# A norm applied behind the products, a fixed start of the program, and the sums of the last pass moved behind the last split

## The chip, the cores and the metric

One core of a Trainium2 chip runs the whole layer; nothing is exchanged with other cores. The metric is the device time of one execution in microseconds (us). The engines are TensorE (PE; its weight loads are shown apart as PEld), VectorE (DVE), ScalarE (ACT), GpSimd (POOL) and SyncE (SP), whose queue issues most of the loads.

## The reference, cut to what matters

A decoder layer over 256 positions with 2048 channels, in float32: a norm, one wide projection that feeds a recurrent branch and an attention branch, their merging, a second norm and an MLP with a norm behind it.

```python
def rmsnorm(x, g):
    y = xf * lax.rsqrt(jnp.mean(xf * xf, axis=-1, keepdims=True) + RMS_EPS)
    return y * g

h = rmsnorm(x, norm_mix_pre[l])
proj = h @ w_in[l]
xr, yr, q, k, v, g_rnn, g_attn = jnp.split(proj, IN_OFFSETS, axis=-1)
xr = rg_lru(causal_depthwise_conv(xr, conv_w, conv_b), ...)
y_rnn = xr * jax.nn.gelu(yr)
q, k = rope(q, positions), rope(k, positions)
y_att = sliding_window_sink_attention(q, k, v, sinks)
mix = sigmoid(g_rnn) * (y_rnn @ w_rnn_proj) + sigmoid(g_attn) * (y_att @ w_attn_proj)
x = x + rmsnorm(mix @ w_out, norm_mix_post)
h = rmsnorm(x, norm_mlp_pre)
u = jnp.square(jax.nn.relu(h @ w_mlp_up))
x = x + rmsnorm(u @ w_mlp_down, norm_mlp_post)
```

The first norm is a factor per position, r = 1/sqrt(mean of x squared + eps), and a gain per channel. The product `h @ w` may therefore be formed as r times the product of (x times gain) with w.

## The kernel before, in words

**Numbers as two parts.** Each float32 weight and activation is split into a high part (rounded to a shorter form that PE takes at full rate, `fp32r`) and a low part (the rest). A product is then three: high by high, high by low, low by high. Weights come as *halves* of 128x1024 from SP's queue (tile `wraw`); ACT casts each into its high part (`whi`, line 92) and DVE subtracts (`wlo`, line 93). `Stream` runs this ahead of the products by up to six halves (`AHEAD`, and six buffers each for high and low parts); a new half can be split when a product has freed a buffer.

**Order.** A scheduler puts the instructions of each engine in an order; `pin` keeps a marked instruction in the written order with other marked ones, and `tc.issue_after(x)` keeps what is inside behind x. Every engine works through its list in order, so an instruction that waits holds up all behind it.

**The head.** The two blocks of 128 positions of x (x0 and x1, 128x2048 each) are loaded, each in two halves, with the first weights between and behind them. Seven products of ones (`warm`, line 342) keep PE at work. The gain of the first norm is one row, loaded on ACT's queue (line 311), that four fp32 products with ones (`gain_b`, line 348) spread over the 128 partitions. For each block ACT and DVE sum the squares of its four quarters (lines 354 and 358), `rms` (lines 334 to 336) makes r out of them, DVE multiplies a quarter by r and the gain in one instruction (line 363), PE transposes it in four 128x128 pieces into a PSUM bank (`ptr`, line 369), ACT casts the high part of the transposed quarter out of it (line 375) and DVE subtracts the low part (line 376). The result, `hT`, feeds all projections. The first of these gives keys and values (bank `kv0` for block 0, `kv1` for block 1; lines 388, 390 and 391), and it is woven by hand into the head. The low parts of the first four weight halves are made by POOL.

**The middle.** Then come, for four groups, the gate `ga` (a product with positions on partitions; its sigmoid is a tanh of half the value) and the queries `q`; behind them the projections x and y (`px`, `py`; eight pairs each, in `conv` and `gelu`, with channels on partitions), the gates of the recurrence, the projections of both branches, `g2`-gates and the merging, the out-projection, the second norm, and the MLP. The keys are rotated by the tables `cc` and `ss` (cosine and sine, made on DVE and ACT from the positions, lines 491 to 510), transposed (`pk`, line 540) and kept for all groups. They are made by a generator, `keys_values`, that the gate's loop steps on.

**The last pass.** The MLP's down-product runs in four passes; `down(f, n, ...)` with f = 1, n = 1 is the last. Seven of its 16 chunk pairs go by Strassen-like sums into the banks P1, P6, Q5 and N7 (named `s` in the profile). When the last of these is in, DVE adds them up into four tiles `ready` (lines 1029 to 1032), `early` adds the first half's sum `acc` to each (line 1094) and loads the last gain `g3`. The last three chunk pairs are held, and are then put into the banks of the four outputs one output after the other (`dQ`, `dCs`, `dP`, `dQ`; line 987). `finish` adds a bank to its `ready` tile (line 1108), sums its squares on ACT (line 1112), multiplies by the gain (lines 1113 and 1118) and, when a block of positions is whole, makes r and writes four outputs (line 1124).

## Time and profile before

| | us |
|---|---|
| median of three runs | 1553.24 (1552.12 to 1554.74) |
| the profiled execution | 1548.21 |
| its span, from the first to the last instruction | 1546.4 |
| PE busy within the span | 1516.1 (98%) |
| DVE busy | 1098.4 (71%) |
| ACT busy | 824.0 (53%) |
| POOL busy | 12.1 (1%) |
| moved from memory | 288.60 MB, 191 GB/s over the span |

The profiled execution is one of its own, apart from the three timed runs; durations below are its durations. A busy share is a mean over all stages. What bounds a stage is read in the timelines, where the bracket behind an instruction gives the time that its engine stood idle before it and what ended that. PE's records can overlap: a product's duration is longer than the step to the next one. In the counts of instructions an fp32 product, or a product of ones, shows as two records.

### The profile page before, as it was taken

The page shows a single profiled execution, that of the slowest core. Times are in us where ns is not written, and L with a number is a line of the kernel's source. Part 1 is how long each engine was busy: PE and PEld are TensorE (multiplying, and loading weights), DVE is VectorE, ACT ScalarE, POOL GpSimd, SP SyncE. Part 2 cuts the span into 40 slices and gives each one's busy share as a digit, 9 for nine tenths or more (in the row PEclk, how much of TensorE's full clock was granted, in tenths as well). Part 3 has the DMA queues.
Part 4 walks back from the last instruction along what each step waited for, and adds up shares of the span by engine and source line. Part 5 has one row for each costly group of instructions (what it writes and reads, how often), then busy time and mean ns, then how long its engine had stood idle before and what let it go on. Part 6 is the DMA issues. An engine that isn't in the chain of part 4 may idle for free.

```text
span 1546.4 us, 19944 instructions
## 1 busy us (share of the span) xinstructions
PE 1516.1 (98%) x7562; PEld 1264.5 (82%) x7562; DVE 1098.4 (71%) x1338; ACT 824.0 (53%) x1116; POOL 12.1 (1%) x14
## 2 busy tenths in 40 slices
PE   7999999999999999999999999999999999999996
PEld 5887777788888888888877888888888888888885
DVE  5666666856759867546666876688886766678897
ACT  4545555646647757444354655555454555555552
POOL 3000000000000000000000000000000000000000
PEclk9999999999999999999999999999999999999999
DMA  6454354354655575665663865556667655576663
GB/s 247 161 179 146 127 174 155 125 185 156 227 193 175 166 222 177 203 196 184 243 237 108 271 202 185 190 182 210 215 205 234 204 188 190 181 282 193 202 212 129
DMA packets 82322, 296.19 MB, mean 192 GB/s; under 512 B 9521, under 2 KB 9777, under 8 KB 81201
## 3 DMA queue, kind: packets, MB, share of 16 engines
q1 hardware_dynamic: 78768, 285.48, 56.6%
q10 hardware_dynamic: 3458, 9.45, 1.6%
q8 instruction: 59, 0.97, 0.2%
q14 instruction: 37, 0.30, 0.1%
HBM read 288.60 MB, written 6.29 MB: 191 GB/s over the span
## 4 chain that ended last, share of the span: by engine, by line
PE 81%; DVE 8%; DMA 5%; ACT 3%; issue 2%; DVEq 0%; POOL 0%; ACTq 0%; SPq 0%; POOLq 0%
PE ps L235 21%; PE ps L238 10%; PE dQ L987 5%; DMA wraw<-in_w_dn 4%; DVE wlo L93 4%; PE dP L987 2%; PE s L987 2%; PE gr L253 2%; PE pa L253 2%; PE pr L257 2%; PE pr L255 2%; PE gr L255 2%; PE q L253 2%; PE pr L253 2%; PE gr L257 2%
## 5 line engine op out<-in xcount | busy, mean ns | idle before, releaser
L93 DVE TENSOR_TENSOR wlo<-wraw,whi 128x1024 fp32r<-128x1024 f32 x524 | 635.3, 1222 | 317.5 <-ACT whi L92 316.4
L92 ACT CAST whi<-wraw 128x1024 fp32r<-128x1024 f32 x528 | 549.3, 1050 | 582.5 <-PE ps L235 140.2
L235 PE MATMUL ps<-h2T,whi 128*128 128x512 f32 x1024 | 256.6, 392 | 0.6 <-DVE h2T L286 0.6
L235 PEld LDWEIGHTS ps<-h2T,whi 128*128 128x128 f32 x1024 | 184.2, 189 | 33.8 <-DVE h2T L286 0.8
L238 PEld LDWEIGHTS ps<-h2T,wlo 128*128 128x128 f32 x1024 | 139.7, 190 | 10.0
L238 PE MATMUL ps<-h2T,wlo 128*128 128x256 f32 x1024 | 142.8, 282 | 0.0
L235 PE MATMUL ps<-hT,whi 128*128 128x512 f32 x512 | 130.2, 394 | 0.0
L987 PE MATMUL dQ<-whi,uT 128*128 128x512 f32 x288 | 106.9, 390 | 0.0
L235 PEld LDWEIGHTS ps<-hT,whi 128*128 128x128 f32 x512 | 91.7, 189 | 18.0 <-issue 1.8
L238 PEld LDWEIGHTS ps<-hT,wlo 128*128 128x128 f32 x512 | 70.0, 190 | 5.0
L238 PE MATMUL ps<-hT,wlo 128*128 128x256 f32 x512 | 71.9, 283 | 0.0
L987 PEld LDWEIGHTS dQ<-whi,uT 128*128 128x128 f32 x288 | 54.2, 188 | 11.3 <-ACT whi L92 0.3
L987 PE MATMUL dQ<-wlo,uT 128*128 128x512 f32 x144 | 56.5, 393 | 4.6 <-DVE wlo L93 4.6
L987 PE MATMUL dCs<-whi,uT 128*128 128x512 f32 x144 | 54.5, 395 | 0.0
L112 DVE TENSOR_TENSOR tlo<-t,thi 128x1536 fp32r<-128x1536 f32 x28 | 49.2, 1756 | 7.3 <-ACT thi L111 7.1
L987 PE MATMUL dP<-whi,uT 128*128 128x512 f32 x144 | 53.8, 389 | 0.0
L253 PE MATMUL ga<-whi,hT 128*128 128x512 f32 x128 | 51.2, 400 | 0.0
L253 PE MATMUL q<-whi,hT 128*128 128x512 f32 x128 | 51.1, 399 | 0.0
L257 PE MATMUL ga<-whi,hT 128*128 128x512 f32 x128 | 50.3, 393 | 0.0
L255 PE MATMUL ga<-wlo,hT 128*128 128x512 f32 x128 | 50.3, 393 | 0.0
L255 PE MATMUL q<-wlo,hT 128*128 128x512 f32 x128 | 50.2, 392 | 0.0
L253 PE MATMUL gr<-whi,hT 128*128 128x512 f32 x128 | 50.0, 391 | 0.0
(272 smaller groups left out, 2581.3 us busy)
## 6 DMA issues: line engine op xcount, KB each, us to landing
wraw<-in_w_up SPq DMA_DIRECT2D x128, 512.0 KB, 4.6
wraw<-in_w_dn SPq DMA_DIRECT2D x128, 512.0 KB, 4.6
wraw<-in_w_g SPq DMA_DIRECT2D x64, 512.0 KB, 4.7
wraw<-in_w_xy SPq DMA_DIRECT2D x64, 512.0 KB, 4.5
wraw<-in_w_q SPq DMA_DIRECT2D x32, 512.0 KB, 4.2
wraw<-in_w_ap SPq DMA_DIRECT2D x32, 512.0 KB, 3.8
wraw<-in_w_rp SPq DMA_DIRECT2D x32, 512.0 KB, 4.4
wraw<-in_w_out SPq DMA_DIRECT2D x32, 512.0 KB, 5.0
```

The lines of the kernel that those rows point to most:

```text
L92: self.pin(self.nc.scalar.copy(hi, src))
L93: self.pin(self.low.tensor_tensor(lo, src, hi.bitcast(F32), ALU.subtract))
L112: v.tensor_tensor(lo, t, hi.bitcast(F32), ALU.subtract)
L235: mm(both, hi[:, k * P : k * P + P], a.rearrange("p a b -> p (a b)"), start=half == 0 and k == 0, stop=False)
L238: mm(ps[:, f, 1, :], lo[:, k * P : k * P + P], a[:, 0, :], start=False, stop=half == 1 and k == 7)
L253: mm(banks[tb][n], a[:, 0, t], hi[:, n * 512 : n * 512 + 512], start=first, stop=False)
L255: mm(banks[tb][n], a[:, 0, t], lo[:, n * 512 : n * 512 + 512], start=False, stop=False)
L257: mm(banks[tb][n], a[:, 1, t], hi[:, n * 512 : n * 512 + 512], start=False, stop=last)
L987: mm(b, a[x], w[y], start=not begun and i == 0, stop=tail and i == 2)
```

## The change

1. *The gain of the first norm* is now a column per tile of 128 channels (`gcol`, 128x16, a new input) and is loaded first on ACT's queue. x is transposed as it is loaded. `quad` (four instructions of 128x128, one block of positions) and `both` (two of 128x256, both blocks) take it out of the PSUM bank and multiply by the gain in the same instruction, high parts on ACT and low parts on DVE. The spreading of the gain is gone, and the scaling of x.
2. *The factor r* is applied behind the products: to the tables `cc` and `ss` (keys and queries), to the values as they are copied, as the scale of the gates' tanh (`rhalf`), and to px and py by a multiplication with `r_all`, which holds r along the free axis for every partition and is made by `spread_r`. The squares are summed behind the kv products, and only one of them in the head.
3. *The order of the head* is pinned throughout: loads, dummies (four more behind the first transposes), the kv products, and four banks by name (`front_bank`) for some of the transposes. All low parts of weights are made by DVE.
4. *In the last pass* all halves are split when the last of the seven is in, and the sums with `acc` and the multiplications with the gain are put behind the last low part.

```diff
-        self.pin(self.low.tensor_tensor(lo, src, hi.bitcast(F32), ALU.subtract))
+        self.last_low = self.pin(self.nc.vector.tensor_tensor(lo, src, hi.bitcast(F32), ALU.subtract))
...
+WARM_ON = 4
...
-    gain = flat(unit("gain", F32))
-    for q in range(4):
-        (nc.gpsimd if q == 3 else nc.vector).memset(gain[:, quarter(q)], 0.0)
-    nc.scalar.dma_start(gain[0:1, :], gains[0:1])
...
+    gcol = const.tile([P, KT], F32, name="gcol")
+    pin(nc.scalar.dma_start(gcol, g_cols))
+
+    def load_x(tb, half):
+        c = slice(half * 1024, half * 1024 + 1024)
+        return pin(nc.sync.dma_start(x_nat[tb][:, c], x_v[tb][:, c]))
+
+    ws.pin_load = pin
+    load_x(0, 0)
+    ws.load_to(1)
+    load_x(1, 0)
+    ws.load_to(4)
+    load_x(0, 1)
+    last = load_x(1, 1)
+    ws.load_to(2 * EXTRA + WRAW)
+    ws.pin_load = lambda i: i
...
-    warm = bank(psb, "warm")
-    for i in range(WARM):
-        mm(warm[:, 0:P], ones, ones, start=True, stop=True)
-    gain_b = []
-    for q in range(4):
-        if q % 2 == 0:
-            room = pair("gain_b")
-        gain_b.append(room[:, q % 2].rearrange("p a b -> p (a b)"))
-        mm(gain_b[q], ones, gain[:, quarter(q)], start=True, stop=True)
+    warm = bank(psm, "warm")
+
+    def dummies(n):
+        for i in range(n):
+            pin(mm(warm[:, 0:P], ones, ones, start=True, stop=True))
...
+    wide_banks = [pair("front") for i in range(2)]
+
+    def front_bank(i):
+        return wide_banks[i % 2][:, i // 2].rearrange("p a b -> p (a b)")
...
-    def scale(tb, q, r):
-        c = quarter(q)
-        pin(nc.vector.scalar_tensor_tensor(x_nat[tb][:, c], x_nat[tb][:, c], r, gain_b[q], ALU.mult, ALU.mult))
...
+    def turn(key, ps, tiles):
+        xT[key] = ps
+        for i, (tb, k) in enumerate(tiles):
+            pin(nc.tensor.transpose(ps[:, i * P : i * P + P], x_nat[tb][:, k * P : k * P + P], ident))
+
+    def act(k, part, t=slice(0, S)):
+        return hT[k // 4][:, k % 4, part, t]
+
+    def quad(tb, q, low):
+
+        t = slice(tb * P, tb * P + P)
         for i in range(4):
             k = 4 * q + i
-            pin(nc.tensor.transpose(ps[:, i * P : i * P + P], x_nat[tb][:, k * P : k * P + P], ident))
-
-    def part(tb, q):
-        t = slice(tb * P, tb * P + P)
-        p3 = ps_t.pop((tb, q)).rearrange("p (a b) -> p a b", a=4)
-        hi = hT[q][:, :, 0, t]
-        pin(nc.scalar.copy(hi, p3))
-        pin(nc.vector.tensor_tensor(hT[q][:, :, 1, t], p3, hi.bitcast(F32), ALU.subtract))
+            src = xT[tb, q][:, i * P : i * P + P]
+            if low:
+                pin(nc.vector.scalar_tensor_tensor(act(k, 1, t), src, gcol[:, k : k + 1], act(k, 0, t).bitcast(F32),
+                                                   ALU.mult, ALU.subtract))
+            else:
+                pin(nc.scalar.activation(act(k, 0, t), src, AF.Copy, scale=gcol[:, k : k + 1]))
+
+    def both(j, low):
+
+        for i in range(2):
+            k = 2 * j + i
+            src = xT[j][:, i * S : i * S + S]
+            if low:
+                pin(nc.vector.scalar_tensor_tensor(act(k, 1), src, gcol[:, k : k + 1], act(k, 0).bitcast(F32),
+                                                   ALU.mult, ALU.subtract))
+            else:
+                pin(nc.scalar.activation(act(k, 0), src, AF.Copy, scale=gcol[:, k : k + 1]))
 
...
+    def kv_hi(j, tb, parts=(0, 1)):
+
+        t = slice(tb * P, tb * P + P)
+        for part in parts:
+            for i in range(2):
+                kt = 2 * j + i
+                pin(mm(kv[tb][0], act(kt, part, t), held[j][0][:, quarter(i)], start=kt == 0 and part == 0,
+                       stop=False))
+
+    def kv_lo(j, tb):
+        t = slice(tb * P, tb * P + P)
+        for i in range(2):
+            kt = 2 * j + i
+            pin(mm(kv[tb][0], act(kt, 0, t), held[j][1][:, quarter(i)], start=False, stop=kt == KT - 1))
+
...
-    square(0, 0)
-    square_v(0, 1)
-    square(0, 2)
-    square_v(0, 3)
-    r = rms(0, 0)
-    ws.low = nc.gpsimd
-    scale(0, 0, r)
-    turn(0, 0)
-    scale(0, 1, r)
-    turn(0, 1)
-    scale(0, 2, r)
-    part(0, 0)
...
+    dummies(WARM)
+    for q in range(2):
+        turn((0, q), bank(psm, "front"), [(0, 4 * q + i) for i in range(4)])
+    dummies(WARM_ON)
+    quad(0, 0, False)
     split(1)
+    quad(0, 0, True)
+    square(0, 0, True)
+    kv_hi(0, 0)
+    for q in range(2):
+        turn((1, q), front_bank(q), [(1, 4 * q + i) for i in range(4)])
+    kv_lo(0, 0)
+    quad(1, 0, False)
+    quad(1, 0, True)
+    kv_hi(0, 1)
     split(2)
+    kv_hi(1, 0)
+    kv_lo(0, 1)
+    kv_lo(1, 0)
+    kv_hi(1, 1)
+    kv_lo(1, 1)
+    for tb in range(TB):
+        quad(tb, 1, False)
     split(3)
+    for tb in range(TB):
+        quad(tb, 1, True)
+    for tb in range(TB):
+        kv_hi(2, tb)
     split(4)
+    for tb in range(TB):
+        kv_lo(2, tb)
+    for j in (4, 5):
+        turn(j, front_bank(j - 2), [(tb, 2 * j + i) for i in range(2) for tb in range(TB)])
+    for tb in range(TB):
+        kv_hi(3, tb)
+    for tb in range(TB):
+        kv_lo(3, tb)
+    for j in (6, 7):
+        turn(j, bank(psm, "front"), [(tb, 2 * j + i) for i in range(2) for tb in range(TB)])
     for j in range(4, 8):
+        both(j, False)
+        split(j + 1)
+        both(j, True)
+        for tb in range(TB):
+            kv_hi(j, tb)
+        for tb in range(TB):
+            kv_lo(j, tb)
...
+    ws.pin = lambda i: i
+    ws.ahead(7)
+    for tb in range(TB):
+        for q in range(4):
+            if tb or q:
+                square(tb, q, q % 2 == 1)
+    r0 = [rms(tb, 0) for tb in range(TB)]
...
+    for tb in range(TB):
+        for t in (cc, ss):
+            nc.vector.tensor_scalar(t[:, tb], t[:, tb], r0[tb], None, ALU.mult)
+    rhalf = small("rhalf", [P, TB])
+    for tb in range(TB):
+        nc.vector.tensor_scalar(rhalf[:, tb : tb + 1], r0[tb], 0.5, None, ALU.mult)
+    r_all = small("r_all", [P, S])
+
+    def spread_r():
+        pr = bank(psm, "pr")
+        for tb in range(TB):
+            dg = t2("dg")[:, 0:P]
+            nc.vector.tensor_scalar(dg, ident, r0[tb], None, ALU.mult)
+            mm(pr[:, tb * P : tb * P + P], ones, dg, start=True, stop=True)
+        nc.scalar.copy(r_all, pr[:, 0:S])
...
-            nc.scalar.copy(v_sb[:, tb, :], banks[tb][:, 256:512])
+            nc.scalar.activation(v_sb[:, tb, :], banks[tb][:, 256:512], AF.Copy, scale=r0[tb])
...
+        spread_r()
...
-            nc.scalar.activation(m1[g][:, tb, :], gate[tb], AF.Tanh, scale=0.5)
+            nc.scalar.activation(m1[g][:, tb, :], gate[tb], AF.Tanh, scale=rhalf[:, tb : tb + 1])
...
         p3 = wide(t2("px"))
         a_pair(hT, p3)
+        nc.vector.tensor_tensor(p3, p3, r_all.unsqueeze(1).to_broadcast([P, 2, S]), ALU.mult)
...
         a_pair(hT, wide(py))
+        nc.vector.tensor_tensor(wide(py), wide(py), r_all.unsqueeze(1).to_broadcast([P, 2, S]), ALU.mult)
...
-            nc.scalar.activation(out[tb], banks[tb], AF.Tanh, scale=0.5)
+            nc.scalar.activation(out[tb], banks[tb], AF.Tanh, scale=rhalf[:, tb : tb + 1])
...
                 if p == SEVEN[-1]:
+                    if f == 1 and n == 1:
+                        ws.split_to(2 * len(chunks))
...
         def early(ready):
-            for (tb, i), t in ready.items():
-                c = quarter(2 * n + i)
-                nc.vector.tensor_tensor(t, t, acc[tb][:, c], ALU.add)
+            with tc.issue_after(ws.last_low.ins) if n == 1 else ExitStack():
+                for (tb, i), t in ready.items():
+                    c = quarter(2 * n + i)
+                    behind = nc.vector.tensor_tensor(t, t, acc[tb][:, c], ALU.add)
+                    if n == 1:
+                        ws.last_low = behind
...
             last[tb, i] = t
             if i == 0:
-                for k in range(2):
-                    c = quarter(k)
-                    nc.vector.tensor_tensor(acc[tb][:, c], acc[tb][:, c], g3[0][:, c], ALU.mult)
+                with tc.issue_after(ws.last_low.ins):
+                    for k in range(2):
+                        c = quarter(k)
+                        nc.vector.tensor_tensor(acc[tb][:, c], acc[tb][:, c], g3[0][:, c], ALU.mult)
...
+        "g_cols": np.ascontiguousarray(per_channel(g("norm_mix_pre"))),
```

In the rows below a name is out<-in with the tile's number where several stand side by side; `x3` counts equal rows, and the bracket has the engines or load queues whose signals the instruction waits for.

The head on PE, before: the gain row's products stand ahead of the first transposes (`ptr`).

```order
L342 MATMUL warm<-ones 128x128 x6
L348 MATMUL gain_b<-gain,ones 128x512 [waits DMAHW2_49,DVE_49]
L348 MATMUL gain_b<-gain,ones 128x512 [waits DVE_49] x2
L348 MATMUL gain_b<-gain,ones 128x512 [waits Pool_49]
L369 MATMUL ptr<-ident,x_76 128x128 [waits DMAHW0_49,DVE_49,Pool_49]
L369 MATMUL ptr<-ident,x_76 128x128 x3
L369 MATMUL ptr<-ident,x_76 128x128 [waits DVE_49]
L369 MATMUL ptr<-ident,x_76 128x128 x3
L390 MATMUL kv_141<-whi_169,hT_137 128x512 [waits Activation_49]
```

The same place now (`front` are the transposes' banks; x_76 is x0, x_77 is x1):

```order
L348 MATMUL warm<-ones 128x128 x6
L369 MATMUL front<-ident,x_76 128x128 [waits DMAHW1_49,Pool_49]
L369 MATMUL front<-ident,x_76 128x128 x3
L369 MATMUL front<-ident,x_76 128x128 [waits DVE_49]
L369 MATMUL front<-ident,x_76 128x128 x3
L348 MATMUL warm<-ones 128x128 x4
L411 MATMUL kv_126<-whi_153,hT_120 128x512 [waits Activation_49]
L411 MATMUL kv_126<-whi_153,hT_120 128x512 x3
L369 MATMUL front<-ident,x_77 128x128 [waits DMAHW3_49]
L369 MATMUL front<-ident,x_77 128x128 x7
```

The first transposes wait for a load and POOL's identity alone. The second four still wait for DVE: of the two banks of their pool one is held by the dummies until the last of them, so they take the bank of the first four, when its four low parts have been taken out.

The keys' place on DVE, now (wlo are low parts of weight halves; L361 are squares, L338 and L340 the norm, L525 `rhalf`, L500 and L503 the beginning of the tables):

```order
L93 TENSOR_TENSOR wlo_370<-wraw_107,whi_369 128x1024 [waits DMAHW1_49,PE_49,Activation_49]
L361 SCALAR_TENSOR_TENSOR j,sqs<-x_76 128x512 x2
L361 SCALAR_TENSOR_TENSOR j,sqs<-x_77 128x512 x2
L338 TENSOR_REDUCE st<-sqs 128x1 [waits DVE_49,Activation_49]
L93 TENSOR_TENSOR wlo_454<-wraw_109,whi_453 128x1024 [waits DMAHW2_49,PE_49]
L340 RECIPROCAL st<-st 128x1 [waits Activation_49]
L338 TENSOR_REDUCE st<-sqs 128x1
L93 TENSOR_TENSOR wlo_482<-wraw_373,whi_481 128x1024 [waits DMAHW7_49,PE_49]
L340 RECIPROCAL st<-st 128x1 [waits Activation_49]
L500 CAST posf<-pos_i 128x2 [waits DMAHW3_49]
L525 TENSOR_SCALAR rhalf<-st 128x1
```

Before, the low part ahead of the tables (L491 there) was followed by them at once. The transposes of the keys (`pk`) stand 67 products behind the first product of `ga`; before they stood 40 behind it.

The last low part on DVE, before (L1029 to L1032 are the sums, L1094 the addition of `acc`, L1118 a multiplication by the gain):

```order
L93 TENSOR_TENSOR wlo_12544<-wraw_12469,whi_12543 128x1024 [waits DMAHW0_49,Activation_49]
L1029 TENSOR_TENSOR t<-s_12047,t 128x512 [waits Activation_49]
L1118 TENSOR_TENSOR acc_11400<-acc_11400,g_12539 128x512 [waits DMAHW2_49]
L1030 TENSOR_TENSOR t<-s_12048,t 128x512 [waits DVE_49,PE_49]
L1094 TENSOR_TENSOR t<-t,acc_11401 128x512
L1031 TENSOR_TENSOR t<-t,s_12048 128x512 [waits DVE_49]
L1032 TENSOR_TENSOR t<-t,s_12048 128x512
L1094 TENSOR_TENSOR t<-t,acc_11400 128x512 [waits DVE_49]
L1094 TENSOR_TENSOR t<-t,acc_11401 128x512 [waits DVE_49]
L1094 TENSOR_TENSOR t<-t,acc_11400 128x512
L93 TENSOR_TENSOR wlo_12548<-wraw_12471,whi_12547 128x1024 [waits DMAHW1_49,Activation_49]
```

And now (L1058 to L1061 are the sums, L1124 the addition of `acc`):

```order
L93 TENSOR_TENSOR wlo_12574<-wraw_12516,whi_12573 128x1024 [waits DMAHW0_49,Activation_49]
L93 TENSOR_TENSOR wlo_12578<-wraw_12518,whi_12577 128x1024 [waits DMAHW1_49,Activation_49]
L1058 TENSOR_TENSOR t<-s_12094,t 128x512 [waits PE_49,Activation_49]
L1059 TENSOR_TENSOR t<-s_12095,t 128x512 [waits DVE_49,PE_49]
L1124 TENSOR_TENSOR t<-t,acc_11448 128x512
L1060 TENSOR_TENSOR t<-t,s_12095 128x512 [waits DVE_49]
L1061 TENSOR_TENSOR t<-t,s_12095 128x512
L1124 TENSOR_TENSOR t<-t,acc_11447 128x512 [waits DVE_49]
```

The last low part follows the one before it at once, and the sums stand behind both.

93 lines of the change are left out of this document (13 added, 80 removed).

## The prediction

> **What bounds the kernel now.** I read the busy time by stage first. The columns of this view are: stretch, its length, then busy time (and count) of PE, PEld, DVE, ACT, POOL, then the granted clock, the DMA share and GB/s.
>
> ```profile
> 0.00:48.24 48.24, 38.17 (x151) 28.75 (x151) 29.61 (x46) 22.29 (x35) 12.07 (x14) 0.93 0.59 219
> 48.24:1517.60 1469.36, 1462.35 (x7354) 1223.72 (x7352) 1048.84 (x1260) 797.59 (x1072) 0.00 (x0) 1.00 0.59 192
> 1517.60:1546.40 28.80, 15.62 (x59) 12.01 (x59) 19.99 (x34) 4.12 (x11) 0.00 (x0) 0.87 0.28 98
> ```
>
> In the middle PE is busy 1462 of 1469 us at a full clock: nothing is to be had there, only to be lost. The head (until the first gate product) and the tail (after the last sums begin) hold 10 and 13 us in which PE does nothing. So I read those two in the timelines (start, duration, instruction, idle time before it and what ended it), the head from the chain of waits on.
>
> ```profile
> 2.75 5.66 DMA gain<-in_gains
> 8.54 5.98 PE L348 MATMUL gain_b<-gain,ones 128*128 128x512 f32 x8 [4.10 <-DMA gain<-in_gains]
> 14.36 1.04 PE L369 MATMUL ptr<-ident,x 128*128 128x128 f32 x8
> 21.83 0.73 PE L388 MATMUL kv<-wlo,hT 128*128 128x512 f32 x2 [1.70 <-POOL wlo L93]
> 24.56 1.12 PE L369 MATMUL ptr<-ident,x 128*128 128x128 f32 x4 [2.00 <-DVE hT L376]
> 25.90 0.63 PE L391 MATMUL kv<-whi,hT 128*128 128x512 f32 x1
> 26.32 0.63 PE L390 MATMUL kv<-whi,hT 128*128 128x512 f32 x1
> 31.38 0.60 PE L369 MATMUL ptr<-ident,x 128*128 128x128 f32 x4
> 31.73 0.47 PE L390 MATMUL kv<-whi,hT 128*128 128x512 f32 x1
> 37.36 0.39 PE L390 MATMUL kv<-whi,hT 128*128 128x512 f32 x1
> 48.24 0.39 PE L253 MATMUL ga<-whi,hT 128*128 128x512 f32 x1
> ```
>
> The head is bound by one row of gains: it lands at 2.75 + 5.66 = 8.41, its fp32 spreading holds PE to 14.52, and only then does a transpose start, at 14.36. After it PE waits twice (1.70 and 2.00) on POOL's low part and DVE. From 37.36 to 48.24 stand 48 products without a wait: **.2267 us a product at the full clock**; at the low one (25.90 to 26.32) .42. Four transposes take .35 at the full clock (31.38 to 31.73), and 1.12 at the low one to their end; less the .25 by which the end laps over what follows (.60 against .35), that is about .21 each.
>
> ```profile
> 1517.60 0.68 DVE L1029 TENSOR_TENSOR t<-s,t 128x512 f32<-128x512 f32 x1
> 1524.06 1.22 DVE L93 TENSOR_TENSOR wlo<-wraw,whi 128x1024 fp32r<-128x1024 f32 x1
> 1525.34 0.79 PE L987 MATMUL dQ<-wlo,uT 128*128 128x512 f32 x1 [4.27 <-DVE wlo L93]
> 1537.67 0.69 DVE L1108 TENSOR_TENSOR acc<-dQ,t 128x512 f32<-128x512 f32 x1 [1.91 <-PE dQ L987]
> ```
>
> The tail is bound by order: the last low part stands behind nine additions on DVE, PE waits 4.27 for it, and the last addition at 1537.67 waits for PE.
>
> **The change, part by part.** It is costed on the profiled execution: span 1546.4, time 1548.21, which lies 5.03 below the median 1553.24 of the runs; I take the difference from one to the other as unchanged.
>
> *Head: gone are the gain row, 8 records of fp32 spreading, the four POOL lows and the scaling of x. Added are 128x128 and 128x256 evacuations with a gain pointer.* Their nearest rows (groups: count, then busy, mean ns, idle):
>
> ```profile
> 4.93 0.63 ACT L354 ACTIVATE j<-x 128x512 f32<-128x512 f32 x1 [2.70 <-DMA x<-in_x]
> 6.16 0.63 ACT L354 ACTIVATE j<-x 128x512 f32<-128x512 f32 x1 [0.50 <-DMA x<-in_x]
> 35.27 5.79 ACT L92 CAST whi<-wraw 128x1024 fp32r<-128x1024 f32 x6
> 36.36 6.91 DVE L93 TENSOR_TENSOR wlo<-wraw,whi 128x1024 fp32r<-128x1024 f32 x6 [0.26 <-ACT whi L92]
> L597 ACT ACTIVATE s<-s,stat 128x128 f32<-128x128 f32 x32 | 12.4, 390 | 1.1 <-DVE stat L591 1.1
> L723 ACT ACTIVATE room<-pg,bh 128x256 f32<-128x256 f32 x32 | 13.0, 478 | 1.5 <-PE pg L720 1.5
> L979 DVE TENSOR_TENSOR e<-e,u 128x128 f32<-128x128 f32 x14 | 4.1, 291 | 0.4
> L687 DVE SCALAR_TENSOR_TENSOR xct<-px,vec,xct 128x255 f32<-128x255 f32 x16 | 7.0, 477 | 0.0
> 1.09 3.35 PE L342 MATMUL warm<-ones 128*128 128x128 f32 x14 [1.09 <-DVE ones L307]
> ```
>
> A high part costs ACT .95 (5.79 less one overlap, over 6), a low part DVE 1.14 (6.91 likewise). Rows that follow each other overlap by about .09, so four evacuations of 128x128 cost ACT 4 x .30 + .09 = 1.29; on DVE I take the plain add's .291 plus .055, the overhead of a scalar operand as between the rows here, pitched .27: four cost 1.15. Pairs of 128x256 cost .86 on both. The chain by these prices:
>
> 1. The first half of x is there at 4.93; four transposes at the low clock end at 6.05. The column gains' load now stands first on ACT, ahead of its table load; issued near .7, when ACT begins, and with the row's 5.66, it is there at 6.4, and I take it as a little earlier. Halves of x and of weights land 1.23 apart (4.93, 6.16), all on SP's queue, so the eight that the head needs first are there by 13.6, each ahead of its use below: the loads do not bound it.
> 2. ACT's four end at 7.35 (7.7 with the late gains), the first high part at 8.35; its low part on DVE at 9.6, the four lows of the activations at 10.7.
> 3. The second group's four transposes wait for those lows, as the order shows (their bank is the one just read), so they end at 11.6; four dummies of two records, .24 each, 13.5; four products, still at the low clock, 15.2; eight transposes of the other block, 16.95.
> 4. ACT goes on: four evacuations to 17.4, the high part 18.35, eight evacuations 20.75, the next high part 21.75. DVE is behind by its low (22.95) and six of the eight activations' lows, 24.65.
> 5. PE does 5 products past that to 25.85 and then waits no more: 16 transposes at .0875 are 1.4, 60 products 13.6, which is 40.85 for the first gate product, 41.2 with a semaphore hop or two. **Against 48.24: −7.0.** The bounds: all waits of step 3 gone, 38.9; every evacuation at the dearer row (.39 and .478 unpitched), 44.
>
> *Clock.* In the stretch here PE was busy 6.3 of 10 us and was granted .67:
>
> ```profile
> 20.00:30.00 10.00, 6.30 (x20) 4.86 (x20) 7.06 (x11) 4.32 (x7) 6.52 (x3) 0.67 0.69 267
> ```
>
> My head has PE as thinly busy until 17; I take the full clock from 17.6, after the dummies and products. The Trainium skill, "TensorE: Matmul & The Clock Gate", Part 4 (PE-mode transpose), says of transposes that the full clock does not engage for them because they do not count as busy in the same way. This trace bears on it only in that its low stretch was partly transposes; by that rule the head would be as in rival B.
>
> *The keys.* The squares, reductions and four scalings of the rope tables now stand between the kv products and k.
>
> ```profile
> 47.49 0.16 DVE L491 CAST posf<-pos_i 128x2 f32<-128x2 int32 x1
> 57.02 0.28 DVE L525 TENSOR_TENSOR k<-ra,rb 128x128 f32<-128x128 f32 x1
> 57.45 0.63 PE L540 MATMUL pk<-ident,k 128*128 128x128 f32 x4
> ```
>
> Before, 9.8 us pass from 47.49 to the end of k at 57.30. Now DVE ends its lows near 41.9 (five at 1.14 behind the last evacuation near 36.2), four squares near 44.7 (one pass over 128x512 and the reading of its sum, taken at .70), reductions, reciprocals and two more lows near 47.9; the table chain with its scalings sets k at 57.7. The transposes of k stand 67 products behind the first gate product: 41.2 + 15.2 = 56.4. PE's transposes, and all products behind them in its fixed order, wait for the difference: **+1.3**. It is 0 if the chain runs without the 1.0 us of idle time that it had, and 3.6 if two more lows, 1.14 each, get between its links.
>
> *The middle.* Two fp32 products, two records each, spread r over the partitions (like the small ones here, .274 a record, and the wait of one evacuation shared out), and 16 multiplications of 128x512 on DVE follow the x and y projections:
>
> ```profile
> L961 PE MATMUL pr<-dg,ones 128*128 128x128 f32 x4 | 0.6, 274 | 0.0
> L243 DVE TENSOR_TENSOR px<-ps,px 128x512 f32<-128x512 f32 x8 | 5.5, 683 | 0.0
> 380.00:400.00 20.00, 20.00 (x115) 17.57 (x115) 18.83 (x27) 12.49 (x17) 0.00 (x0) 1.00 0.63 206
> ```
>
> The products are **+.4**. The multiplications are 16 x .60 to .71 = 9.6 to 11.4 us of DVE; the last stretch, amid the x and y projections, has DVE 94% busy (18.83 of 20), and PE loses nothing in it. What covers them is the run-ahead: up to six halves of weights stand split ahead of PE, and each feeds it with 12 products' worth, 2.7 us, so a multiplication that holds up one low part by .7 reaches PE only when the store is empty. That DVE still has some 6% to give, 1.2 us in 20, against two multiplications in each such stretch (1.2 to 1.4), is why I do not put zero. I put **+.5**, between 0 and 2; without the cover it is 11.4 (rival D).
>
> *Tail.* The last low part goes ahead of the sums. Its high part lands where it did:
>
> ```profile
> 1517.19 1.05 ACT L92 CAST whi<-wraw 128x1024 fp32r<-128x1024 f32 x1 [0.28 <-DMA wraw<-in_w_dn]
> 1519.86 0.68 DVE L1030 TENSOR_TENSOR t<-s,t 128x512 f32<-128x512 f32 x1
> 1520.46 0.68 DVE L1094 TENSOR_TENSOR t<-t,acc 128x512 f32<-128x512 f32 x1
> 1530.97 0.16 DVE L334 TENSOR_REDUCE st<-sqs 128x1 f32<-128x4 f32 x1
> 1531.69 1.42 DVE L1124 SCALAR_TENSOR_TENSOR x<-acc,st,x 128x512 f32<-128x512 f32 x2
> 1534.35 0.68 DVE L1108 TENSOR_TENSOR acc<-dP,t 128x512 f32<-128x512 f32 x1
> ```
>
> High ready 1518.24, low done 1519.5. PE has some 56 products behind it: 1519.5 + 12.7 = 1532.4, which alone would be −5.2. But DVE: the 16 operations of 128x512 that stood between 1517.60 and 1530.97 at .60 each (1519.86 to 1520.46) are 9.6, from 1519.42 with two dependencies 1529.2; the norm .72 (1530.97 to 1531.69), four outputs 2.66 (1531.69 to 1534.35): 1532.6; the additions of dP and their product 1.35: the last addition near 1533.95 instead of 1537.67. **−3.7**, set by DVE (−3.4 to −4.4).
>
> Sum: −7.0 + 1.3 + .4 + .5 − 3.7 = **−8.5**: profiled 1539.7, and against the median **1544.7**, −.55%.
>
> **The rivals.**
> *A, the column gains come late.* 128 rows of 64 bytes instead of one of 8 KB. If they land as the row did, at 8.41, step 1 ends 2.3 later and nothing makes it good: −6.2, 1547.0. For it: that load took 5.66 for 8 KB. Against: it is now issued first.
> *B, the clock opens later.* If the transposes do not count, the 5 products and first four transposes after 24.65 run low: 5 x .20 + 4 x (.21 − .09) = 1.5; with all 16 transposes low 3.0. That is 1546.2 to 1547.7. For it: .67 in a stretch with transposes; against: the dummies and products in between.
> *C, the keys' wait is larger.* Lows of the gate's halves stand between the chain's links on DVE, and each waits for a high part that waits for PE to free a buffer. If the wait grows by 4, three or four such lows: −4.5, 1548.7. For it: nothing on PE is free to go ahead of the transposes; against: the order puts just five lows there, two more than before, and both are in the sum.
> *D, the slower side: the multiplications are exposed.* Each holds up ACT's use of px or py and the low part behind it; if the run-ahead is used up in these stages PE waits for all 16: 11.4 instead of .5 gives +2.4, 1555.6. It decides from about 9.0 of the 11.4 on. For it: DVE at 94% in the stretch above, before anything is added; against: PE waits nowhere in it, so the store of halves is not empty now, and the stages between have DVE less busy to fill it again (1049 of 1469 over the middle).
> *E, the banks do not do what they are to:* the second group waits on DVE all the same; that is in the sum already, and without the wait step 3 would be 2 us better at most, 1542.7.
>
> **How the numbers follow.** Forecast .56, A .12, B .12, C .09, D .06, E .05. About 3.1 us (.2%) is what a measurement of this kernel tells from no change. Bounds of the terms reach 1540 and 1551.6; the ends 1541.0 and 1550.0 leave about one in ten on either side. Faster: all but D and the far ends of B and C, .87; within .2% .08; slower .05 (D together with a wait of C).
>
> **What would show it.** The first gate product near 41; evacuations of 128x128 near .39 and .35; no wait on DMA before the first of them (else A); the granted clock 1.0 from 18 on (else B); PE idle one to two us before the transposes of k (else C); no new idle time of PE at the x and y projections (else D); the last low part ending near 1 us behind its high part, and the last addition bound by DVE, not PE. I am wrong if the head does not come to 41 ± 2.5, or the middle loses over 3 us.

## The result and the profile after

The change makes the kernel faster: 1541.47 us (median of four runs, 1539.51 to 1542.65) against 1552.68 for the kernel before beside it, a ratio of **.9927, interval .9912 to .9942**. That is 11.2 us where 8.5 were forecast. The profiled execution took 1541.55 us, its span is 1539.8.

The busy time by stage, cut where the stages of the change begin (same columns as in the prediction; head, middle, from the first of the last sums on):

```profile
0.00:40.56 40.56, 33.92 (x151) 27.86 (x151) 22.76 (x41) 22.05 (x40) 1.70 (x9) 1.00 0.64 240
40.56:1516.46 1475.90, 1466.21 (x7361) 1225.52 (x7359) 1064.91 (x1302) 801.74 (x1082) 0.00 (x0) 1.00 0.59 193
1516.46:1539.80 23.34, 12.99 (x56) 10.44 (x56) 18.40 (x33) 3.48 (x10) 0.00 (x0) 0.83 0.26 90
```

The head is 7.7 us shorter (48.24 before). The middle ends elsewhere in the two kernels, since the sums now wait for the last low parts, so the 6.5 us by which it is longer are not a loss as they stand: 1.1 of them lie between the first gate product and the merging, 2.5 between the merging and the last sums' product, in code that the change does not touch, and 2.9 between that product and the first of the sums. Two granted clocks in these rows need care. The record of the clock begins only at 16.29 in this profile, and the view counts what lies ahead of it as 1.00; that PE ran slower there is seen in two rows of eight transposes each:

```profile
14.84 1.75 PE L369 MATMUL front<-ident,x 128*128 128x128 f32 x8
25.14 1.04 PE L369 MATMUL front<-ident,x 128*128 128x128 f32 x8
```

And the .83 of the last row comes from a fall at 1531.81, behind PE's last product. The timeline of PE's head, and what ACT and DVE hand to it:

```profile
4.96 1.09 PE L369 MATMUL front<-ident,x 128*128 128x128 f32 x4 [0.53 <-DMA x<-in_x]
6.09 1.14 ACT L384 ACTIVATE hT<-front,gcol 128x128 fp32r<-128x128 f32 x4 [3.43 <-PE front L369]
7.10 1.06 ACT L92 CAST whi<-wraw 128x1024 fp32r<-128x1024 f32 x1
9.34 1.12 DVE L381 SCALAR_TENSOR_TENSOR hT<-front,gcol,hT 128x128 fp32r<-128x128 f32 x4
10.51 1.11 PE L369 MATMUL front<-ident,x 128*128 128x128 f32 x4 [4.46 <-DVE hT L381]
12.98 2.05 PE L411 MATMUL kv<-whi,hT 128*128 128x512 f32 x4
40.56 0.39 PE L254 MATMUL ga<-whi,hT 128*128 128x512 f32 x1
```

The first transposes start with x, nothing waits for the gains, and the one long wait that is left (4.46) is that of the second four transposes for their bank. In the tail the last low part follows its high part, and the last addition, on DVE, comes without a wait:

```profile
1514.24 1.05 ACT L92 CAST whi<-wraw 128x1024 fp32r<-128x1024 f32 x1 [1.39 <-DMA wraw<-in_w_dn]
1515.32 1.23 DVE L93 TENSOR_TENSOR wlo<-wraw,whi 128x1024 fp32r<-128x1024 f32 x1 [1.21 <-ACT whi L92]
1516.60 0.50 PE L1014 MATMUL dQ<-wlo,uT 128*128 128x512 f32 x1 [0.77 <-DVE wlo L93]
1529.19 0.39 PE L1014 MATMUL dQ<-whi,uT 128*128 128x512 f32 x1
1530.96 0.68 DVE L1140 TENSOR_TENSOR acc<-dQ,t 128x512 f32<-128x512 f32 x1
```

PE ends 1.4 us ahead of the addition (1529.58 against 1530.96): DVE is the bound here, as the prediction had it.

### The profile page after: what moved, and what is told of

Same layout as the page of the kernel before. It is cut to its first block, busy times and chain, and to the rows that moved or that the text cites. A ratio compares the mean times of both kernels' runs of the same rounds, so it can differ in the third digit from the quotient of the medians.

```text
span 1539.8 us, 19994 instructions
## 1 busy us (share of the span) xinstructions
PE 1513.1 (98%) x7566; PEld 1263.8 (82%) x7566; DVE 1106.1 (72%) x1373; ACT 827.3 (54%) x1131; POOL 1.7 (0%) x9
## 4 chain that ended last, share of the span: by engine, by line
PE 85%; DVE 6%; DMA 4%; ACT 2%; issue 2%; DVEq 0%; SPq 0%; ACTq 0%
PE ps L236 22%; PE ps L239 11%; PE dQ L1014 6%; PE s L1014 3%; PE dP L1014 3%; DMA wraw<-in_w_dn 3%; DVE wlo L93 2%; PE dCs L1014 2%; PE gr L254 2%; PE gr L258 2%; PE pr L258 2%; PE pr L254 2%; PE pa L258 2%; PE q L254 2%; PE pr L256 2%; PE pa L254 2%
```

## The experiments

### The kernel before, again

No edit.

> The kernel before once more, unchanged. Between the two profiles the change is worth 6.7 us of execution time (1548.21 to 1541.55), between the medians 11.2. Theory: the profiled execution of before was a quick one of its own spread; a second profile of it lies at 1551 to 1554, with the surplus of 3 to 6 us in places that the change does not touch (waits for weight loads in the MLP), and head and tail as in the first profile (first gate product at 48.2 +- 0.3, last addition 23.4 us behind the end of the last sums' products, +- 0.5). Rival: the surplus lies in the head or the tail, whose waits vary from run to run; then the first gate product or the last low part moves by 3 us or more. The timed ratio to before is 1.000 within 0.2% in both.

Ratio .9999 (.9989 to 1.001); the profiled execution took 1553.49 us, its span is 1551.7. The first gate product stands at 47.61, .6 us earlier than in the first profile: outside the ± .3 of the first theory, and far from the 3 us of the rival. The tail, from the start of the last sums' product to the last addition, is 25.3 us long (23.6 in the first profile), more than expected. From PE's first transposes of the merging, near 750 us, to the start of the last sums' product (1514.04 in the first profile, 1517.37 here) it is 763.5 us in the first profile and 767.5 in this one, in code that the change does not touch. Of these 4.0 us, 2.0 are waits of PE in the MLP for tiles that DVE makes (.9, .9 and .6, against .4 in all in the first profile), and 1.3 are in the second norm. There it shows by a stretch of 20 us, first profile, then this one:

```profile
828.00:848.00 20.00, 16.31 (x96) 12.86 (x95) 17.77 (x29) 11.03 (x21) 0.00 (x0) 1.00 0.17 52
```

```profile
828.00:848.00 20.00, 16.54 (x84) 13.20 (x84) 17.62 (x26) 12.03 (x22) 0.00 (x0) 0.83 0.23 69
```

With PE waiting a good 3 us in both, the granted clock fell in one and not in the other (.83 as a mean), and PE got through 84 products instead of 96. So the profile on which the prediction stood was a quick one: a difference between two single profiles can carry some 4 us of chance from code that the change leaves alone, and here another 1.7 from the tail.

### The head alone

The three hunks in the last pass are undone:

```diff
-                    if f == 1 and n == 1:
-                        ws.split_to(2 * len(chunks))
...
-            with tc.issue_after(ws.last_low.ins) if n == 1 else ExitStack():
-                for (tb, i), t in ready.items():
+            for (tb, i), t in ready.items():
...
-                with tc.issue_after(ws.last_low.ins):
-                    for k in range(2):
+                for k in range(2):
```

> The change without its part in the last pass (the split of all halves, the sums and multiplications behind the last low part). Theory, by the profiles: the head gives 7.7, the middle takes part of it back, the tail gives about 3: this kernel is 6 to 8.5 us faster than before and 3 to 4 slower than the whole change, and its last low part again stands behind the additions, with PE waiting some 4 us for it. Rival: the head's gain is lost in the middle, whose waits for weight loads set the pace, and most of the 11 us comes from the tail: then it is at most 4 us faster than before.

Ratio .9952 (.9937 to .9968): 7.4 us faster than before. The first theory holds for the time. Its detail on the tail was too large: the last low part stands behind the additions again, but PE waits 1.88 for it, not 4. Between the last two low parts DVE takes 5.6 us and not 6.5, as it does not wait for the gain there (.97 in the first profile of before), and PE's ten products of the second output ahead of that wait run in part at a clock of .5 (from 1512.95 to 1516.36).

### The tail alone

The same three hunks, put into the kernel before (with the line that keeps the last low part).

> The kernel before with the change's part in the last pass alone. Theory: 3 to 4 us faster than before, the last low part about 1.2 us behind its high part, the last addition waiting for DVE and not for PE. Rival: the last weight loads land later than they are wanted now and take it back (in the profile of the change PE waits .77, .45 and .77 for the last parts): 1 to 2 us. If the two parts add up, this and the head alone together make 11 us within 1.5.

Ratio .9976 (.9965 to .9988): 3.7 us. With the head's 7.4 that makes 11.1, and the whole change, run again below, 11.0: the parts add up. In the profile of this run the last addition waits for PE after all:

```profile
1520.52 1.04 ACT L92 CAST whi<-wraw 128x1024 fp32r<-128x1024 f32 x1 [2.41 <-DMA wraw<-in_w_dn]
1521.60 1.23 DVE L93 TENSOR_TENSOR wlo<-wraw,whi 128x1024 fp32r<-128x1024 f32 x1 [2.23 <-ACT whi L92]
1521.62 0.79 PE L987 MATMUL dQ<-whi,uT 128*128 128x512 f32 x1 [1.46 <-ACT whi L92]
1538.51 0.69 DVE L1113 TENSOR_TENSOR acc<-dQ,t 128x512 f32<-128x512 f32 x1 [1.20 <-PE dQ L987]
```

The last half landed late (2.41 of waiting for the load), PE's products then took .79 instead of .50, the clock being low, and PE ended behind DVE. Which of the two sets the end thus differs from run to run, and it goes with the clock. Eleven profiles here have the tail in its new order. The clock fell for 6.83 us ahead of PE's last product in four of them (this one, two with another head, and one with POOL at work in the tail), and there the last addition waits for PE, by .63 to 1.35 us. It fell for 3.41 us in two (a wait of .20 in one, none in the other) and not at all in five, where DVE sets the end.

### Without the multiplications by r

```diff
-        nc.vector.tensor_tensor(p3, p3, r_all.unsqueeze(1).to_broadcast([P, 2, S]), ALU.mult)
...
-        nc.vector.tensor_tensor(wide(py), wide(py), r_all.unsqueeze(1).to_broadcast([P, 2, S]), ALU.mult)
```

> The change without the 16 multiplications of px and py by r (128x512 on DVE): px and py are left unscaled, so this part of the computation is left out. Theory: DVE's multiplications are covered by the halves split ahead, so at most 1 us is gained against the whole change (11 to 12.5 faster than before), although DVE is busy 10 us less. Rival, D of the prediction: they are exposed and 6 to 11 us are gained on top. Between profiles, the stages of the x and y projections show which: with the theory they take the same time within .5 us.

Ratio .9939 (.9924 to .9954), against .9927 and .9929 for the whole change: nothing is gained that can be measured, and the 9.5 us are fewer than the 11 to 12.5 expected. The profiles show a small price, at the edge of the .5 us that the theory allowed. The last row of the head and the first transposes of the merging, in the change and then without the multiplications:

```profile
40.56 0.39 PE L254 MATMUL ga<-whi,hT 128*128 128x512 f32 x1
...
743.93 0.38 PE L836 MATMUL ptr<-ident,kept 128*128 128x128 f32 x2
```

```profile
39.80 0.39 PE L254 MATMUL ga<-whi,hT 128*128 128x512 f32 x1
...
742.57 0.38 PE L834 MATMUL ptr<-ident,kept 128*128 128x128 f32 x2
```

That is 703.37 with and 702.77 without them, so .6 us for 16 instructions that keep DVE busy for 11.0 (8 of 687 ns and 8 of 691):

```profile
L723 DVE TENSOR_TENSOR py<-py,r_all 128x512 f32<-128x512 f32 x8 | 5.5, 691 | 0.2
L706 DVE TENSOR_TENSOR px<-px,r_all 128x512 f32<-128x512 f32 x8 | 5.5, 687 | 0.0
```

Rival D falls: they are covered to some 95%. (The .6 rests on one profile without them.)

### The whole change, again

> The whole change once more, beside the kernels of this call. The theory that the parts add up: head alone .9952 and tail alone .9976 of before make .9928, about 11 us; measured first .9927. Rival: the profiles' 6.7 us are the true size and the first four runs were lucky ones: .9955. Its profile should show the first gate product at 40.6 +- 1.5 (the clock's opening moves by up to 2 us from run to run), and the keys' transposes without a wait.

Ratio .9929 (.9916 to .9943): 11.0 us, so the first measurement stands and the rival, the profiles' 6.7, falls. The first gate product is at 40.07, and from there to the transposes of the merging it is 703.33 us, .04 from the first profile; before it was 702.28 and 702.30. The stage is that steady, and the change's price in it, some 1.05 us, is well measured. One profile stands out: with the head alone it is 703.95, .46 of it because the keys' transposes came that much later and waited for DVE there.

### A bank of its own for the second four transposes

```diff
-    warm = bank(psm, "warm")
...
+    warm = front_bank(3)
```

> The change with the dummies' bank taken from the named banks (it is the one that the fourth of them needs much later), so that the second four transposes get a bank of their own pool at once. Theory, from the profile of the change: these transposes, 4.46 us late, hold up the four dummies and with them the first products (12.98, though their high part was ready at 8.16); without that wait the first products begin near 8.2, the other block's transposes near 11.5 instead of 14.84, and the first gate product comes 2.5 to 4 us earlier. The keys' transposes may then wait for DVE's chain, and give 0 to 2 back. Timed: 1 to 3.5 us faster than the whole change. Rival, E of the prediction: 2 us at most in the head. Second rival: PE idles between instead, the clock opens later and nothing is gained.

The wait of 4.46 is gone, and the first products begin as soon as their high part is there:

```profile
5.02 1.94 PE L369 MATMUL front<-ident,x 128*128 128x128 f32 x8 [0.58 <-DMA x<-in_x]
6.76 1.25 PE L346 MATMUL front<-ones 128*128 128x128 f32 x8
8.28 0.74 PE L411 MATMUL kv<-whi,hT 128*128 128x512 f32 x2 [0.27 <-ACT whi L92]
10.40 1.03 PE L369 MATMUL front<-ident,x 128*128 128x128 f32 x8
35.66 0.39 PE L254 MATMUL ga<-whi,hT 128*128 128x512 f32 x1
```

The head is 4.4 to 4.9 us shorter than in the two profiles of the change, twice what rival E allowed. A part of this that is not told apart is the clock's, which opened at 7.15 here and at 16.29 and 15.20 there. Timed it is .9923 (.9911 to .9936), 1 us better than the change beside it at .9929, with intervals that overlap. Against the first profile of the change most of the head's gain is given back where the clock falls, 1.3 us in the second norm and 2.9 in the tail. The second norm (twenty us) and the tail (ten), in this kernel, then the same two stretches in the change (the second of them from its second profile):

```profile
820.00:840.00 20.00, 16.56 (x93) 13.23 (x92) 17.15 (x25) 11.49 (x20) 0.00 (x0) 0.91 0.31 100
1511.00:1521.00 10.00, 6.62 (x17) 4.82 (x18) 9.16 (x14) 2.12 (x3) 0.00 (x0) 0.77 0.28 100
```

```profile
820.00:840.00 20.00, 16.29 (x93) 12.68 (x92) 16.89 (x28) 11.45 (x22) 0.00 (x0) 1.00 0.12 36
```

```profile
1511.00:1521.00 10.00, 10.00 (x45) 8.26 (x45) 9.53 (x18) 1.75 (x5) 0.00 (x0) 1.00 0.00 2
```

Whether an earlier head makes the clock fall more often there, or it was chance, these runs don't settle.

### The head in another order

With the bank as above. Of the rest the first moves are shown, and the squares that go to ACT.

```diff
     for q in range(2):
         turn((0, q), bank(psm, "front"), [(0, 4 * q + i) for i in range(4)])
-    dummies(WARM_ON)
     quad(0, 0, False)
-    split(1)
     quad(0, 0, True)
-    square(0, 0, True)
-    kv_hi(0, 0)
+    split(1)
     for q in range(2):
         turn((1, q), front_bank(q), [(1, 4 * q + i) for i in range(4)])
+    kv_hi(0, 0)
...
+    square(0, 0)
+    square(0, 1)
+    square(1, 0)
+    square(1, 1)
```

> The same, and the head in another order: the other block's transposes stand ahead of the first products, the four later dummies are left out, low parts of activations stand ahead of those of weights where both are due, and four of the eight squares are summed on ACT while it would wait in the head. Theory: from about 9 us on PE waits no more, 96 products and 16 transposes at the full clock are 23.4, with some 6 us of them at half clock 2.5 more: the first gate product near 35.5 to 37, 4 to 5 us earlier than with the change, and 3 to 5 faster when timed. Rival: DVE's chain for the keys, not PE, then sets the pace, and the gain beyond that of the bank alone is under .7 us.

Ratio .9911 (.9895 to .9926): 2.7 us faster than the change beside it by the medians (1537.64 against 1540.29), the fastest kernel by then. The first gate product stands at 35.64, where it was forecast, and PE waits no more from 8.24 on. It is there no earlier than with the bank alone (35.66), but the clock was not the same: with the bank alone it stayed at 1.0 from 7.15 on, and here it fell to .5 from 7.52 to 14.35. Two kernels further below, with dummies and with all three additions, have this same head. By the stretch from 8 to 16 us, in this kernel, with all three additions, and with the dummies in the second norm:

```profile
8.00:16.00 8.00, 7.76 (x26) 6.50 (x27) 6.57 (x17) 6.61 (x18) 0.00 (x0) 0.60 1.02 411
```

```profile
8.00:16.00 8.00, 7.23 (x30) 6.26 (x31) 6.20 (x16) 6.08 (x16) 0.00 (x0) 0.79 1.02 413
```

```profile
8.00:16.00 8.00, 7.43 (x37) 6.30 (x38) 7.14 (x18) 6.96 (x19) 0.00 (x0) 1.00 1.02 414
```

Their first gate products stand at 35.64, 34.64 and 33.09, in the order of the clock. So with the clock at 1.0 the other order gives 2.6 us beyond the bank (33.09 against 35.66), and the rival, under .7 us, holds only for a profile in which the clock fell. The medians differ by 1.4 us; their intervals overlap.

### POOL for four multiplications of the tail

```diff
-                        nc.vector.tensor_tensor(acc[tb][:, c], acc[tb][:, c], g3[0][:, c], ALU.mult)
+                        nc.gpsimd.tensor_tensor(acc[tb][:, c], acc[tb][:, c], g3[0][:, c], ALU.mult)
```

> The change with the four multiplications of acc by the last gain on POOL instead of DVE (same instruction on another engine). Theory: the end is set by DVE now; without these four (4 x .60 = 2.4 us) the last addition waits for PE, whose last product ends 1.4 us before it: 1.2 to 1.5 us faster than the whole change, with the last addition's idle time ended by PE. Rival: POOL is late with them (its low parts of 128x1024 took 2.4 to 2.6 us in the kernel before, so 1.3 for one of these, 5.2 in all) and holds up the outputs of the first block, or slows DVE beside it: no gain, or slower.

Ratio .9934 (.9921 to .9946), no gain. POOL does them in 5.93 us beside DVE, and DVE's additions take 1.60 us meanwhile that take .69 in the change:

```profile
1517.22 5.93 POOL L1151 TENSOR_TENSOR acc<-acc,g 128x512 f32<-128x512 f32 x4 [1514.89 <-ACT t L1057]
1519.17 1.60 DVE L1124 TENSOR_TENSOR t<-t,acc 128x512 f32<-128x512 f32 x1
1520.69 0.67 DVE L1060 TENSOR_TENSOR t<-t,s 128x512 f32<-128x512 f32 x1
1521.29 0.67 DVE L1061 TENSOR_TENSOR t<-t,s 128x512 f32<-128x512 f32 x1
1521.89 3.02 DVE L1124 TENSOR_TENSOR t<-t,acc 128x512 f32<-128x512 f32 x3
```

In the change:

```profile
1517.86 0.69 DVE L1124 TENSOR_TENSOR t<-t,acc 128x512 f32<-128x512 f32 x1
1519.65 1.90 DVE L1124 TENSOR_TENSOR t<-t,acc 128x512 f32<-128x512 f32 x3
```

The second half of the rival holds: 2.0 of the 2.4 us that DVE was to save (.91 and 1.12) are lost in these four additions. The two additions between them, which read one operand from a PSUM bank (`s`), keep their .67 us beside POOL. The last addition does wait for PE, as the theory has it (.63), but the clock was at .5 for 6.83 us in this tail. The Trainium skill, "Perfetto Trace Analysis", Optimizing Scalar/DVE Operations, says that GpSimd and VectorE share a read port to SBUF, so that moving work between these two may not help; the run agrees, at .9 us for one addition and POOL multiplication (1.48 on the mean) that overlap.

### The column gains later

```diff
-    pin(nc.scalar.dma_start(gcol, g_cols))
...
     pin(nc.scalar.activation(st[:, 31:32], eps, AF.Sqrt))
+    pin(nc.scalar.dma_start(gcol, g_cols))
```

> The change with the load of the column gains issued behind ACT's first activation instead of ahead of it (about 1.9 us later, near 2.7). It prices rival A of the prediction. In the profile of the change ACT's first evacuation waits for PE's transposes (6.09), not for the gains, so they land in at most 5.4 us. Theory: they then land between 6 and 8.4, the first evacuation moves from 6.09 by 0 to 2.3, and the first gate product by the same: timed 0 to 2.3 us slower than the change, .9927 to .9945 of before. Rival: the load is quick (under 3.5 us) and nothing moves.

The edit did not do what it was for: the load is issued at .90 instead of .73, ahead of the activation's end at 2.23, and the first evacuation again waits for PE. Ratio .9943 (.9925 to .9961), which is not told apart from the change. What a late landing would cost was not tried further. In every profile of a kernel with the column gains, ACT's first evacuation waits for PE and not for the load.

### Dummies in the second norm

Added to the other order of the head: 5, 3 and 5 dummies behind the first three groups of the last block's transposes.

```diff
                 transpose_split(h2[tb], h2T, tb, q, room[:, q % 2].rearrange("p a b -> p (a b)"))
+                if tb == 1:
+                    for i in range(HOLD[q]):
+                        pin(mm(warm, ones, junk[:, 0:P], start=True, stop=True))
```

> The head in the other order with its bank, as before, and 13 more dummies between the last transposes of the second norm. In five of nine profiles so far the granted clock fell to .5 there for 3.4 or 6.8 us, and the stage was 1.2 to 2.3 us longer. Theory: the dummies keep the clock at 1.0 there and give what the fall costs on the mean, about 1 us: .990 to .991 of before. Rival: they stand in the way of the transposes, or the clock falls all the same: no gain over .9911, or slower.

Ratio .9908 (.9892 to .9924) after .9911: no gain that can be told. (By a count of all profiles up to then it is five of ten, not of nine.) The clock stays at 1.0, but from the merging's first transposes (row of 743.93 above) to the first small products of the second norm (tile `pr`) it is now 127.0 us, against 125.8 in the order without the dummies, where the clock did fall. They hold the clock, and the stage is no shorter: the first half of the rival fits, that they stand in the way of the transposes.

### Products of zeros in the tail, and all three

```diff
+                    if held == 3 and name == order[0] and (p, i) in FILL:
+                        for k in range(FILL[p, i]):
+                            mm(banks[b], zero, zmove, start=False, stop=False)
```

with four each ahead of the last three halves.

> The change with twelve products of zeros (four each ahead of the last three halves' products of the first output, added into its bank), where PE waits about 2 us for the last weight halves. In the profiles so far the time from the last sums' product to the last addition was 20.4 to 21.0 where the granted clock stayed at 1.0 there or fell for 3.4 us, and 23.2 to 24.5 where it fell for 6.8 us. Theory: with PE kept at work the clock stays at 1.0, the last addition waits for DVE in every run, and the mean gains .5 to 2 us (.9915 to .9925 of before), with 20.4 to 21.2 in the profile. Rival: the zeros delay the real products by up to 2.7 us where the halves come in time, and nothing is gained.

> Three additions to the change together: the head's other order with its bank, the dummies in the second norm, and the products of zeros in the tail. Theory: .9890 to .9905 of before, the first gate product at 33 to 36, the tail 20.4 to 21.2. Rival: the head and the second norm alone are all of it, .9908 as measured, or more.

Alone: .9935 (.9918 to .9951); all three: .9912 (.9896 to .9927). Both ratios lie above what the theories forecast (the intervals reach into it), and that nothing is gained fits both rivals. In both profiles the clock stays at 1.0 up to PE's last product and the last addition comes 20.8 us behind the last sums' product, as the theory has it; but so it did in the two profiles of the change (21.0 and 20.4), and on the mean nothing is gained. Nothing here beats the order of the head alone, which with or without the dummies is about 14 us (.9908 to .9911) faster than before.

## Why the prediction was right

**Direction and size.** Measured 1541.47, inside 1541.0 to 1550.0 but close to its lower end; forecast 1544.7. The likeliest case came, with one term too dear and one too small. By its terms, first profile against first profile unless said:

- *Head, −7.0:* −7.7, and −7.5 from second to second profile (47.61 to 40.07). Five more profiles with this head have the first gate product at 39.7 to 39.8, and one more with the head of before at 48.1: on the mean of all, −8.1 (47.99 to 39.92). The chain came link by link: transposes to 6.05 (6.05 forecast), first high part 8.16 (8.35), the lows 10.46 (10.7), the second four transposes 11.6 (11.6), the first four products from 12.98 (13.5). The prices for the evacuations, taken from other instructions, fit:

```profile
L384 ACT ACTIVATE hT<-front,gcol 128x128 fp32r<-128x128 f32 x16 | 4.5, 391 | 11.2 <-PE front L369 11.2
L395 ACT ACTIVATE hT<-front,gcol 128x256 fp32r<-128x256 f32 x8 | 3.4, 477 | 4.0 <-PE front L369 4.0
L381 DVE SCALAR_TENSOR_TENSOR hT<-front,gcol,hT 128x128 fp32r<-128x128 f32 x16 | 4.4, 344 | 6.0 <-ACT hT L384 6.0
```

- *The keys, +1.3:* nothing (with the head alone .46). This is the term that was wrong, at its lower bound (which, without the 1.0 us of idle time, comes to .3 and not to the 0 that is written). PE's transposes of k follow the 67 products without a wait (40.56 + 67 x .2267 = 55.75):

```profile
46.10 0.15 DVE L500 CAST posf<-pos_i 128x2 f32<-128x2 int32 x1
55.22 0.28 DVE L549 TENSOR_TENSOR k<-ra,rb 128x128 f32<-128x128 f32 x1
55.75 0.60 PE L564 MATMUL pk<-ident,k 128*128 128x128 f32 x4
```

  DVE's chain ended at 55.50, not 57.7. Most of the 2.2 is in its start, 1.8: the tables began at 46.10 instead of 47.9, as the lows ended at 41.0 (41.9 forecast), the four squares took .61 and not .70 each, and the two lows behind them 2.7 and not 3.2 with the norm. The other .4 is the tables', 9.4 against 9.8.
- *Spreading and multiplications, +.4 and +.5:* 1.05 in all, steady over the profiles, of which .6 belong to the multiplications, by the one profile without them.
- *The tail, −3.7:* 3.7 when timed alone. Between the first profiles only 2.6 (from the last sums' product to the last addition, 23.6 and 21.0), as the last half's high part began 1.1 us later behind that product; between the second ones 4.9 (25.3 and 20.4). In the prediction's sum for PE alone 1519.5 + 12.7 is 1532.2, not 1532.4, and one of the nine "additions" ahead of the old last low part is a multiplication; the −3.7 rests on neither. DVE is the bound while the clock holds. That PE can become it again, when the clock falls behind a late half, the prediction did not see.
- *The sum:* with the head of all profiles, 8.1 less 1.05 and 3.7 more are 10.7 (10.2 to 10.4 by the pairs), against 11.2 and 11.0 measured, within their intervals of some 2 us either way. Of the 2.7 us between forecast and result the keys are 1.3 and the head .5 to 1.1; for the rest no place is shown. Taking over the 5.03 us between the profiled execution and the median as unchanged did no harm, since every term is a difference within a stage. But the profiled execution of the change lies on its own median: the gap was that one profile's luck, most of it in code that the change does not touch.
- *The middle:* the prediction calls itself wrong if it loses over 3 us. From the first gate product to the last sums' product the first pair of profiles says 3.6 us more (1465.8 to 1469.4), the second pair 5.2 less (1469.8 to 1464.6). A single pair can't decide that sign; the 1.05 above are what repeats.

**The rivals.** A did not come (no profile has ACT waiting for the gains). B did not: the clock opened, and stayed open, from 16.3 in the first profile and 15.2 in the second, against 17.6 assumed. C did not, D fell by experiment, and E was priced too low at 2 us: with the bank the head gains over 4 and ends at 35.66, below the prediction's own bound of 38.9 without that wait, since not the transposes alone stood behind it but the dummies and the first products as well, and the clock opened earlier. The rule of the Trainium skill behind B, "TensorE: Matmul & The Clock Gate", Part 4 (PE-mode transpose), that transposes do not count as busy in the same way, is not borne out by the run with the bank. There the record of the clock begins at 7.15, with 1.0, and the dummies around it start .21 us apart until then and .11 from there. Of the 2.83 us that PE was busy in the 3.41 before (the clock's recorded stretches are multiples of 3.41 us) only the first .7 and the last .4 were dummies, and the rest transposes. The 1.00 of the first row is again time ahead of the record:

```profile
3.74:7.15 3.41, 2.83 (x14) 2.56 (x13) 0.00 (x0) 1.00 (x4) 0.00 (x0) 1.00 0.98 340
7.15:10.56 3.41, 2.35 (x14) 1.58 (x13) 2.30 (x6) 1.07 (x2) 0.00 (x0) 1.00 1.02 412
```

The kernel with the dummies in the second norm agrees (clock 1.0 from 6.56, behind 2.83 us busy, 1.5 of it with transposes), and so does that with all three additions (from 11.55, behind 2.78, 1.6 of it with transposes). In the other order of the head 2.69 us, 1.6 of it with transposes, were followed by a clock of .5. What decides between these is not shown.

## What to carry to other kernels

Walk the chain of a start-up link by link with prices from the nearest rows, and name the bank or buffer that each link waits for: that gave the head within .6 to 1.5 us, and the one wait left in the plan (a bank held by dummies) was worth over 4 us of the head in the profile without it, though the timed runs show only 1 us of it, within their intervals. A factor that moves behind a product costs DVE time, not time, while a run-ahead of several halves stands between DVE and PE: 11.0 us of work cost .6. And before a sum is set against a median, take a second profile: here two of the same kernel differ by 5.3 and 5.9 us, 4.0 and 4.8 of them between the merging and the last sums, which the change leaves alone.

## What had not been expected of the hardware

- In the two places where PE waits for two or three microseconds behind the head, the granted clock falls to .5 for 3.41 or 6.83 us in some profiles and stays at 1.0 in others: in the second norm it fell in five of the first ten (from the merging's first transposes to that norm's small products the five without took 123.8 to 125.3 us, the five with 124.5 to 126.6); in the tail it goes with whether PE or DVE ends last. Keeping PE busy with dummies or zeros held the clock at 1.0 at its place in all four cases, in three profiles, in which it was tried, and no time was gained that could be measured.
- How much POOL slows DVE: an addition of two 128x512 tiles on DVE takes 1.60 us instead of .69 while POOL multiplies such tiles, and one that reads a PSUM bank for one of them does not (.67). The kernel before shows the slowing too, in its head, where POOL made low parts: two equal passes over 128x512 there take 1.25 and 2.83 us, as against .69 without POOL.

```profile
18.31 1.25 DVE L358 SCALAR_TENSOR_TENSOR j<-x 128x512 f32<-128x512 f32 x1
19.49 2.83 DVE L358 SCALAR_TENSOR_TENSOR j<-x 128x512 f32<-128x512 f32 x1
```
